# Splitting the next weights behind the eviction of the last finished product, in one encoder layer on one core

## The chip, the core and the metric

The kernel runs on one core of a Trainium2 chip. Five engines work side by side, each with a queue of its own that it takes in order: PE (TensorE, the matmuls), DVE (VectorE), ACT (ScalarE), POOL (GpSimd) and SP (SyncE, which here issues most DMAs). An engine that meets an instruction whose inputs are not ready waits with everything behind it. The metric is the time of one execution on the device, in microseconds (us). It was 2259.2, 2258.1 and 2256.8 us in three runs, a median of 2258.14 us.

## What is computed

One layer of an encoder, in float32, on two inputs with the same weights: `x_prompt` (1024 tokens of width 1024), called A below, and `x_sample` (512 tokens), called B. Cut to what matters:

```python
def encoder_layer(x, ...):
    h = rms_norm(x, pre_w)
    cols = h @ w_in                       # q|k, v, o, z, gates of the mLSTM; q, k, v, z of the attention; merge gates
    m_qk, m_v, m_o, m_z, m_i, m_f, a_qkv, a_z, gate = split(cols)
    y_m = mlstm_mixer(m_qk, m_v, m_o, m_i, m_f, ...) * silu(m_z)     # both directions, chunks of 128 tokens
    y_a = dilated_attention(a_qkv, rel_table) * silu(a_z)            # 3 dilations, 8 heads of 64
    p_m = y_m @ w_proj_m
    p_a = y_a @ w_proj_a
    g = sigmoid(gate)
    merged = g[0] * p_m + g[1] * p_a
    return x + rms_norm(merged @ w_out, post_w)
```

The mLSTM is a recurrence over chunks: each step takes a matrix state (`cf` in the kernel), adds the product of keys and values of the chunk to it, and divides by a denominator that follows from it.

## The kernel before

[...] Each operand is held as a high part, rounded, and a low part, the rest; `mm3` (L206) issues high × high, high × low and low × high (lines L209, L210, L211), and leaves out low × low.

**Weights.** A tile of weights is 128 x 1024 float32. `load_w` (L255) has it brought by a DMA into one of two buffers `wraw`; the queue is SP's, and POOL's in the later stages. `split_w` (L264) makes the high part with ACT (L272, `wh`) and the low part with DVE (L278, `wl`), into one of three pairs of buffers (in some stages there are more: `X0`, `X1`, `Q1`). Loading and splitting run two tiles of weights ahead of the products.

**Products.** `unit` (L792) multiplies one tile of weights with the activations of 512 tokens: 8 steps of `mm3` into one PSUM bank called `dense`, of which the scans' stage has two. Then `use(ps)` evicts the finished product, that is, ACT or DVE read the bank and so give it back: `silu` (ACT's tanh, L746, and DVE's product, L749 or L751), `att_unit` (ACT's copy, L772, and DVE's low part, L774), `conv` (ACT's copy, L870), `gate` (ACT's tanh, L896), and in the last stages `proj_m`, `proj_a` and `close`.

**Stages.** To about 950 us the projections of A with `w_in`, with a scheme of products of their own; from 973 to 1330 us the scan of A's mLSTM, with the projections of B set between its steps; to about 1600 us the attention of A with further projections; then the scan of B (to about 1830 us); then the attention of B beside the products with `w_proj_m` and `w_proj_a` (`w_pm`, `w_pa`), and the last product with `w_out`.

**A step of the scan** takes `rm` (POOL L1103, ACT L1105, DVE L1106), `sch`/`scl` (ACT L1109, POOL L1110), `kh`/`kl` (ACT L1124, DVE L1125), `qh`/`ql` (ACT L1117, POOL L1118); PE then writes `num` (two PSUM banks) and `kv` (one). DVE reads `kv` into the state `cf` (L1149, L1152); ACT and DVE read `num` into `X` (L1167, L1169), with a reciprocal `r` (L1163, L1164); ACT and DVE then split the state again (`ch` L1176, `cl` L1177). `hn` (ACT L1182, L1185) and `r` (POOL L1183, L1184) norm the heads.

**A step of the attention** takes the logits `lg` (PE L1362), their maximum with a bias into `ls` and `ot` (DVE L1374, `ISA` in the lists below), `nm` (DVE L1376), the exponential (ACT L1378), a transpose (`pt`, PE L1385), its copy (`pts`, ACT L1388 or DVE L1390) and the product `o` (PE L1398). `K0`, `K1` are the high and low part of rows `ymr` that POOL loads (L250, L1594, L1595).

**What sets the order.** The order on PE and on SP is that of the code, written by hand. On ACT, DVE and POOL a scheduler sets it, which takes each instruction's turn from a model of the timeline. `issue_after(x)` gives it a further condition: what is issued under it comes after `x`. Between instructions of one engine that is a place in the queue and costs no semaphore. `split_w` uses it already: both parts come after the instructions in `self.held` (in the attention, the last four steps' reads of PSUM), the low part also after those in `self.scans` (in the scan, the last reads of `kv` and `num`).

Of the kernel before, what the change touches and what calls it, by code (L numbers as in the profile page):

```python
# [22 lines left out]
F32 = mybir.dt.float32  # L23
# [158 lines left out]
class Net:  # L182
    def __init__(self, tc, a):
        self.tc, self.nc, self.a = tc, tc.nc, a
        self.clock = self.lag = 0
        self.pending, self.owner = [], {}
        self.defer, self.mixed, self.rows = False, set(), {}
        self.queued, self.pace = [], 1
        self.side = self.nc.sync
        self.lows = None  # L190
        self.scans, self.state, self.held, self.sum = [], [], [], None
        self.low_part = None
        self.retired = []
        self.narrow, self.acc, self.direct = {}, [None, None], {}
# [69 lines left out]
    def split_w(self, raw, n):  # L264
# [4 lines left out]
        with ExitStack() as st:  # L269
            for x in self.held:  # L270
                st.enter_context(self.tc.issue_after(x.ins))
            high = nc.scalar.activation(hi[:, :n], raw[:, :n], AF.Copy)  # L272

        def rest():
            with ExitStack() as st:
                for x in (*self.held, *self.scans):
                    st.enter_context(self.tc.issue_after(x.ins))
                low = (self.lows or nc.vector).tensor_sub(lo[:, :n], raw[:, :n], hi[:, :n].bitcast(F32))  # L278
# [463 lines left out]
    def silu(self, c, g, w):  # L742

        nc = self.nc
        th = w()
        nc.scalar.activation(th, c, AF.Tanh, scale=0.5)  # L746
        if g is None:
            g = th
            nc.vector.scalar_tensor_tensor(g, th, 1.0, c, op0=OP.add, op1=OP.mult)  # L749
        else:  # L750
# [9 lines left out]
    def att_unit(self, j, c, T, w):  # L760
# [10 lines left out]
        for h, _, x in parts:  # L771
            nc.scalar.activation(h, x, AF.Copy, scale=1.0 if keys else 0.125)  # L772
        for h, l, x in parts:
            nc.vector.scalar_tensor_tensor(l, x, 1.0 if keys else 0.125, h.bitcast(F32), op0=OP.mult, op1=OP.subtract)  # L774
        self.put(("aqk", T.S, j), T.aqk[0, j], hi.bitcast(F32), hi)
# [86 lines left out]
    def short_units(self, T):  # L862
# [5 lines left out]
        def conv(u):  # L868
            def use(p):
                nc.scalar.activation(self.sraw[:, 1:1 + BLK], p, AF.Copy)  # L870
                self.conv_unit(u, T, self.sraw, w, False)
# [21 lines left out]
        def gate(br, ct):  # L893
            def use(p):
                t = w()
                nc.scalar.activation(t, p, AF.Tanh, scale=0.5)  # L896
                self.put(("gt", T.S, br, ct), T.gt[br, ct], t, t)
# [719 lines left out]
    def branches(self, T, b, odd, before):  # L1617
# [12 lines left out]
        def proj_m(weights):  # L1630
            m2[:] = [self.place(1 - odd, i, F32) for i in (0, 2)]
            gate(1, 0)
            for ct in range(KT):
                wm = weights()
                pm = self.dense()
                for k in range(KT):
# [5 lines left out]
                    if k == KT - 1:  # L1642
                        nc.vector.scalar_tensor_tensor(m2[ct // 4][:, ct % 4], gates.pop((1, ct)), 1.0, pm, op0=OP.add, op1=OP.mult)  # L1643
                    yield

        def proj_a(weights):
            for ct in range(KT):
# [5 lines left out]
                for k in range(4):  # L1653
# [4 lines left out]
                    if k == 3:  # L1658
                        mg = self.osb.tile([P, BLK], F32, name="mg", bufs=2)
                        nc.vector.scalar_tensor_tensor(mg, gates.pop((0, ct)), 1.0, pa, op0=OP.add, op1=OP.mult)  # L1660
                        nc.vector.tensor_add(mg, mg, m2[ct // 4][:, ct % 4])
# [20 lines left out]
    def final(self, T, b):  # L1682
# [4 lines left out]
        def make(weights):  # L1687
# [13 lines left out]
            def close(u, t, c, p):  # L1701
                r0 = b * BLK + t * P
                o1 = sb.tile([P, BLK], F32, name="mg", bufs=2) if u else o[t]
                nc.scalar.activation(o1, p, AF.Square, accum_out=ss[:, t, u:u + 1])
                if u == 0:
                    nc.vector.tensor_mul(o[t], p, pw[:, c])
                    return
                which, xt = xo[t]
                nc.vector.scalar_tensor_tensor(ss[:, t, 5:6], ss[:, t, 0:1], 4 * EPS * D, ss[:, t, 1:2], op0=OP.add, op1=OP.add)
                nc.gpsimd.tensor_tensor(ss[:, t, 6:7], ss[:, t, 5:6], self.mhalf[:, :1], op=OP.pow)  # L1710
                nc.vector.tensor_mul(o1, p, pw[:, c])
                for hf, x in enumerate((o[t], o1)):
# [338 lines left out]
```

## Time and profile before

| | |
|---|---|
| median of three runs | 2258.14 us |
| the profiled execution | 2261.5 us, its span 2259.7 us |
| PE busy | 2244.2 us, 99% of the span |
| DVE, ACT, POOL busy | 1509.5, 1129.2 and 718.6 us |
| bytes moved by DMA | 418.27 MB, 185 GB/s |

The span is the time from the first to the last instruction that the profiler recorded; 1.8 us of the execution lie around it. An instruction in the trace has a start, a duration, its engine, its line and what it writes and reads; the names of buffers are shown without their numbers there. In square brackets stands the idle time of the engine ahead of it, with what ended it. PE's idle time is the difference of its busy time and the span, 15.5 us in all.

### The profile page before, as it was taken

The numbers are of one execution on the slowest core, as the hardware profiler recorded it, in microseconds if no ns is written. First come the engines' busy times: TensorE is split into PE (matmuls) and PEld (weight loads), VectorE is DVE, ScalarE is ACT, GpSimd is POOL, SyncE is SP. The second block draws the span as 40 slices with busy tenths as digits, with TensorE's granted clock in tenths as the row PEclk, the third lists the DMA queues.
The fourth block names the chain that finished last, engine by engine and source line by source line (L and its number), as shares of the span: only waits on it lengthen the run. The fifth ranks groups of instructions, "written<-read, shape, count | busy, mean of one in ns | idle before, by whom it ended". The sixth has DMA issues, their size and how long they took to land.

```text
span 2259.7 us, 35388 instructions
## 1 busy us (share of the span) xinstructions
PE 2244.2 (99%) x12226; PEld 1964.6 (87%) x12226; DVE 1509.5 (67%) x2875; ACT 1129.2 (50%) x2369; POOL 718.6 (32%) x1000
## 2 busy tenths in 40 slices
PE   9999999999999999999999999999999999999998
PEld 8999888888888888888888899999888888888887
DVE  7765577687776556558887755544689844655674
ACT  6432244344444434357777655566665644554332
POOL 1000333333333223237676610011165522221221
PEclk9999999999999999999999999999999999999999
DMA  3652455543332223284664789997678797776663
GB/s 123 168 134 76 172 205 192 192 176 121 112 111 103 84 84 140 103 298 153 226 223 127 191 217 235 253 245 221 203 248 284 238 278 211 233 251 200 233 230 109
DMA packets 222685, 418.27 MB, mean 185 GB/s; under 512 B 24841, under 2 KB 128969, under 8 KB 222506
## 3 DMA queue, kind: packets, MB, share of 16 engines
q1 hardware_dynamic: 194536, 315.86, 44.4%
q0 software_dynamic: 24368, 87.56, 12.4%
q10 hardware_dynamic: 3602, 12.59, 1.4%
q8 instruction: 97, 1.59, 0.3%
q14 instruction: 82, 0.67, 0.1%
HBM read 296.19 MB, written 128.12 MB: 188 GB/s over the span
## 4 chain that ended last, share of the span: by engine, by line
PE 95%; DMA 2%; issue 1%; ACT 1%; POOL 1%; DVE 0%; DVEq 0%; SPq 0%; POOLq 0%; ACTq 0%
PE d L211 14%; PE d L209 14%; PE d L210 14%; PE dense L209 12%; PE dense L211 12%; PE dense L210 12%; PE o L1398 4%; PE pt L1385 2%; PE lg L1362 2%; PE num L211 1%; PE num L209 1%; PE num L210 1%; PE kv L209 1%; PE a L1070 1%; PE kv L210 1%
## 5 line engine op out<-in xcount | busy, mean ns | idle before, releaser
L209 PE MATMUL dense<-H,wh 128*128 128x512 f32 x664 | 270.6, 408 | 0.8 <-DVE V0b L1643 0.8
L211 PE MATMUL dense<-H,wl 128*128 128x512 f32 x664 | 260.9, 393 | 0.0
L210 PE MATMUL dense<-H,wh 128*128 128x512 f32 x664 | 260.2, 392 | 0.0
L210 PE MATMUL d<-Hl,phla 128*128 128x512 f32 x608 | 236.5, 389 | 0.0
L211 PE MATMUL d<-Hh,phla 128*128 128x512 f32 x608 | 236.5, 389 | 0.0
L209 PE MATMUL d<-Hh,phla 128*128 128x512 f32 x608 | 236.5, 389 | 0.0
L278 DVE TENSOR_TENSOR wl<-wraw,wh 128x1024 fp32r<-128x1024 f32 (+1 forms) x121 | 149.3, 1234 | 70.0 <-ACT wh L272 69.9
L1374 DVE CUSTOM_DVE_ANT_0 ls<-lg,bias 128x256 f32<-128x256 f32 (+1 forms) x288 | 93.7, 362 | 132.8 <-PE lg L1362 71.2
L211 PE MATMUL d<-Hh,phlb 128*128 128x512 f32 x456 | 177.4, 389 | 0.0
L209 PE MATMUL d<-Hh,phlb 128*128 128x512 f32 x456 | 177.4, 389 | 0.0
L210 PE MATMUL d<-Hl,phlb 128*128 128x512 f32 x456 | 177.4, 389 | 0.0
L687 POOL TENSOR_TENSOR psum_w<-pw_raw 128x512 f32<-128x512 f32 x38 | 58.0, 1527 | 365.1 <-DMA pw_raw<-w_in 208.8
L1378 ACT ACTIVATE ls<-ls,nm 128x256 f32<-128x256 f32 (+1 forms) x288 | 130.3, 454 | 84.0 <-DVE nm L1376 59.2
L272 ACT ACTIVATE wh<-wraw 128x1024 fp32r<-128x1024 f32 (+1 forms) x124 | 128.7, 1038 | 77.1 <-PE dense L210 27.0
L211 PEld LDWEIGHTS dense<-H,wl 128*128 128x128 f32 x664 | 124.6, 188 | 28.2
L209 PE MATMUL d<-vhi,Hh 128*128 128x322 f32 x448 | 140.9, 315 | 0.3
L211 PE MATMUL d<-vhi,Hl 128*128 128x322 f32 x448 | 140.3, 313 | 0.4 <-DVE Hl L396 0.2
L210 PE MATMUL d<-vlo,Hh 128*128 128x322 f32 x448 | 139.7, 312 | 0.0
L209 PEld LDWEIGHTS dense<-H,wh 128*128 128x128 f32 x664 | 125.0, 188 | 15.5 <-DVE V0b L1643 1.2
L210 PEld LDWEIGHTS dense<-H,wh 128*128 128x128 f32 x664 | 125.4, 189 | 14.3
L211 PEld LDWEIGHTS d<-Hh,phla 128*128 128x128 f32 x608 | 114.1, 188 | 23.7
L210 PEld LDWEIGHTS d<-Hl,phla 128*128 128x128 f32 x608 | 114.2, 188 | 23.6
(570 smaller groups left out, 6166.4 us busy)
## 6 DMA issues: line engine op xcount, KB each, us to landing
pw_raw<-w_in SPq DMA_DIRECT2D x76, 512.0 KB
wraw<-w_in SPq DMA_DIRECT2D x64, 512.0 KB
aqk_a<-pwk SPq DMA_DIRECT2D x48, 512.0 KB
aqk_b<-sw SPq DMA_DIRECT2D x48, 256.0 KB
wraw<-w_pm POOLq DMA_DIRECT2D x24, 512.0 KB, 6.1
wraw<-w_out POOLq DMA_DIRECT2D x24, 512.0 KB, 4.0
wraw<-w_v POOLq DMA_DIRECT2D x22, 430.0 KB, 7.3
erep<-erow SPq DMA_DIRECT2D x16, 512.0 KB
```

The lines of the kernel that those rows point to most:

```text
L209: nc.tensor.matmul(out, lh, rh, start=start, stop=False)
L210: nc.tensor.matmul(out, lh, rl, start=False, stop=False)
L211: nc.tensor.matmul(out, ll, rh, start=False, stop=stop)
L272: high = nc.scalar.activation(hi[:, :n], raw[:, :n], AF.Copy)
L278: low = (self.lows or nc.vector).tensor_sub(lo[:, :n], raw[:, :n], hi[:, :n].bitcast(F32))
L687: self.nc.gpsimd.tensor_add(s[:, 0], ws[1][:, 0], ws[1][:, 1])
L1070: nc.tensor.matmul(p[:, c - c0], kT[:, ct, c * P:(c + 1) * P], qT[:, ct, c * P:(c + 1) * P], start=ct == 0, stop=ct == 1)
L1362: nc.tensor.matmul(lg[:, hh, c:c + w], q[hh][:, qs], z[:, k0:k0 + w], start=z is k[hh], stop=z is not k[hh])
L1374: nc.vector.tensor_tensor_reduce(out=ls[:, hh], in0=ts["lg"][hh], in1=bt[:, hh], scale=1.0, scalar=NEG, op0=OP.add, op1=OP.max, accum_out= ...
L1378: self.held = self.held[-3:] + [nc.scalar.activation(ls[:, hh], ls[:, hh], AF.Exp, bias=nm[:, hh:hh + 1], accum_out=ot[:, 128 + hh:129 + hh])]
L1385: nc.tensor.transpose(pp[:, hh * nk + x], ts["ls"][:, hh, x * P:(x + 1) * P], self.ident)
L1398: nc.tensor.matmul(po[:, hh * 64:hh * 64 + 64], pt[:, hh * nk + x], v[:, kt[x], c0 + hh * 64:c0 + hh * 64 + 64], start=x == 0, stop=x == n ...
```

## The change

A new list `self.evicted` holds the instructions on ACT and DVE that evict the last finished product. Each `use` sets it anew. `split_w` puts both the high part and the low part behind what the list holds, in addition to `held` and `scans`. Since the condition is only one of order on the same engine, the high part comes after ACT's entries and the low part after DVE's.

```diff
--- before.py
+++ after.py
@@ -189,7 +189,7 @@
         self.side = self.nc.sync
         self.lows = None
         self.scans, self.state, self.held, self.sum = [], [], [], None
-        self.low_part = None
+        self.low_part, self.evicted = None, []
         self.retired = []
         self.narrow, self.acc, self.direct = {}, [None, None], {}
 
@@ -267,13 +267,13 @@
         hi, lo = self.wsplit.pop(0)
         self.wsplit.append((hi, lo))
         with ExitStack() as st:
-            for x in self.held:
+            for x in (*self.held, *self.evicted):
                 st.enter_context(self.tc.issue_after(x.ins))
             high = nc.scalar.activation(hi[:, :n], raw[:, :n], AF.Copy)
 
         def rest():
             with ExitStack() as st:
-                for x in (*self.held, *self.scans):
+                for x in (*self.held, *self.evicted, *self.scans):
                     st.enter_context(self.tc.issue_after(x.ins))
                 low = (self.lows or nc.vector).tensor_sub(lo[:, :n], raw[:, :n], hi[:, :n].bitcast(F32))
             self.splits = high, low
@@ -743,10 +743,10 @@
 
         nc = self.nc
         th = w()
-        nc.scalar.activation(th, c, AF.Tanh, scale=0.5)
+        self.evicted = [nc.scalar.activation(th, c, AF.Tanh, scale=0.5)]
         if g is None:
             g = th
-            nc.vector.scalar_tensor_tensor(g, th, 1.0, c, op0=OP.add, op1=OP.mult)
+            self.evicted.append(nc.vector.scalar_tensor_tensor(g, th, 1.0, c, op0=OP.add, op1=OP.mult))
         else:
             nc.vector.scalar_tensor_tensor(g, th, 1.0, g, op0=OP.add, op1=OP.mult)
         return g
@@ -769,9 +769,10 @@
             by = lambda z: z.rearrange("p (r i) -> p r i", r=dil)
             parts = [(by(hi), by(lo), c.rearrange("p (i r) -> p r i", r=dil))]
         for h, _, x in parts:
-            nc.scalar.activation(h, x, AF.Copy, scale=1.0 if keys else 0.125)
+            self.evicted = [nc.scalar.activation(h, x, AF.Copy, scale=1.0 if keys else 0.125)]
         for h, l, x in parts:
-            nc.vector.scalar_tensor_tensor(l, x, 1.0 if keys else 0.125, h.bitcast(F32), op0=OP.mult, op1=OP.subtract)
+            low = nc.vector.scalar_tensor_tensor(l, x, 1.0 if keys else 0.125, h.bitcast(F32), op0=OP.mult, op1=OP.subtract)
+        self.evicted.append(low)
         self.put(("aqk", T.S, j), T.aqk[0, j], hi.bitcast(F32), hi)
         self.put(("aqk", T.S, j), T.aqk[1, j], lo.bitcast(F32), lo)
 
@@ -867,7 +868,7 @@
 
         def conv(u):
             def use(p):
-                nc.scalar.activation(self.sraw[:, 1:1 + BLK], p, AF.Copy)
+                self.evicted = [nc.scalar.activation(self.sraw[:, 1:1 + BLK], p, AF.Copy)]
                 self.conv_unit(u, T, self.sraw, w, False)
             return self.unit(u, use)
 
@@ -893,7 +894,7 @@
         def gate(br, ct):
             def use(p):
                 t = w()
-                nc.scalar.activation(t, p, AF.Tanh, scale=0.5)
+                self.evicted = [nc.scalar.activation(t, p, AF.Tanh, scale=0.5)]
                 self.put(("gt", T.S, br, ct), T.gt[br, ct], t, t)
             return self.unit((U_GB, U_GA)[br] + ct, use)
 
@@ -1640,7 +1641,8 @@
                     if k == 3:
                         gate(*((1, ct + 1) if ct < KT - 1 else (0, 0)))
                     if k == KT - 1:
-                        nc.vector.scalar_tensor_tensor(m2[ct // 4][:, ct % 4], gates.pop((1, ct)), 1.0, pm, op0=OP.add, op1=OP.mult)
+                        self.evicted = [nc.vector.scalar_tensor_tensor(m2[ct // 4][:, ct % 4], gates.pop((1, ct)), 1.0, pm,
+                                                                       op0=OP.add, op1=OP.mult)]
                     yield
 
         def proj_a(weights):
@@ -1657,7 +1659,7 @@
                         gate(0, ct + 1)
                     if k == 3:
                         mg = self.osb.tile([P, BLK], F32, name="mg", bufs=2)
-                        nc.vector.scalar_tensor_tensor(mg, gates.pop((0, ct)), 1.0, pa, op0=OP.add, op1=OP.mult)
+                        self.evicted = [nc.vector.scalar_tensor_tensor(mg, gates.pop((0, ct)), 1.0, pa, op0=OP.add, op1=OP.mult)]
                         nc.vector.tensor_add(mg, mg, m2[ct // 4][:, ct % 4])
                         nc.scalar.activation(mh[:, ct % 4], mg, AF.Copy)
                         nc.vector.tensor_sub(ml[:, ct % 4], mg, mh[:, ct % 4].bitcast(F32))
@@ -1701,14 +1703,14 @@
             def close(u, t, c, p):
                 r0 = b * BLK + t * P
                 o1 = sb.tile([P, BLK], F32, name="mg", bufs=2) if u else o[t]
-                nc.scalar.activation(o1, p, AF.Square, accum_out=ss[:, t, u:u + 1])
+                self.evicted = [nc.scalar.activation(o1, p, AF.Square, accum_out=ss[:, t, u:u + 1])]
                 if u == 0:
-                    nc.vector.tensor_mul(o[t], p, pw[:, c])
+                    self.evicted.append(nc.vector.tensor_mul(o[t], p, pw[:, c]))
                     return
                 which, xt = xo[t]
                 nc.vector.scalar_tensor_tensor(ss[:, t, 5:6], ss[:, t, 0:1], 4 * EPS * D, ss[:, t, 1:2], op0=OP.add, op1=OP.add)
                 nc.gpsimd.tensor_tensor(ss[:, t, 6:7], ss[:, t, 5:6], self.mhalf[:, :1], op=OP.pow)
-                nc.vector.tensor_mul(o1, p, pw[:, c])
+                self.evicted.append(nc.vector.tensor_mul(o1, p, pw[:, c]))
                 for hf, x in enumerate((o[t], o1)):
                     c2 = slice(hf * BLK, (hf + 1) * BLK)
                     nc.vector.scalar_tensor_tensor(xt[hf], x, ss[:, t, 6:7], xt[hf], op0=OP.mult, op1=OP.add)
```

The names below have the buffers' numbers, and lines after the change are one or two higher than before (L1185 is L1186).

On ACT at about 1057 us of the profile before, in the scan of A, where `wh0` is the high part of the next weights, `sw2` the eviction of a product and `hn3` a step of the head norm, there stood

```order
L1182 ACTIVATE hn3_7909,r_8888<-X0_7911 128x256
L1109 ACTIVATE sch_8994<-rm_8988 128x128
L272 ACTIVATE wh0_7755<-wraw0_7753 128x1024
L772 ACTIVATE sw2_7873<-dense_8805 128x512
L1185 ACTIVATE hn3_7909<-X0_7911,r_8888 128x256
L1105 ACTIVATE rm_9107<-rm_9107,col1024_715 128x128
L1124 ACTIVATE kh_9117<-K1_8196,col1024_715 128x256
```

and now stand

```order
L1183 ACTIVATE hn3_7909,r_8888<-X0_7911 128x256
L1110 ACTIVATE sch_8994<-rm_8988 128x128
L772 ACTIVATE sw2_7873<-dense_8805 128x512
L1186 ACTIVATE hn3_7909<-X0_7911,r_8888 128x256
L272 ACTIVATE wh0_7755<-wraw0_7753 128x1024
L1106 ACTIVATE rm_9107<-rm_9107,col1024_715 128x128
L1125 ACTIVATE kh_9117<-K1_8196,col1024_715 128x256
```

The eviction now comes ahead of the split, and so does the second `hn3`; the rows behind are the same. On DVE at about 1287 us, late in the same scan, where `sg` is the eviction's second half (it reads ACT's `sw3`) and `cf1` the state, there stood

```order
L1163 SCALAR_TENSOR_TENSOR r_12057<-num_12030,col1024_715 128x1
L1164 RECIPROCAL r_12057<-r_12057 128x1
L1169 SCALAR_TENSOR_TENSOR X0_7911<-num_12030,r_12057,X0_7911 128x256
L1177 TENSOR_TENSOR cl0_12062<-cf0_11384,ch0_12061 128x516
L1152 SCALAR_TENSOR_TENSOR cf1_11444<-cf1_11444,rw1_7903,kv_12105 128x516
L751 SCALAR_TENSOR_TENSOR sg_7877<-sw3_7874,sg_7877 128x512
L1125 SCALAR_TENSOR_TENSOR kl_12155<-K1_10377,col1024_715,kh_12154 128x256
```

and now stand

```order
L1164 SCALAR_TENSOR_TENSOR r_12057<-num_12030,col1024_715 128x1
L1165 RECIPROCAL r_12057<-r_12057 128x1
L1170 SCALAR_TENSOR_TENSOR X0_7911<-num_12030,r_12057,X0_7911 128x256
L1178 TENSOR_TENSOR cl0_12062<-cf0_11384,ch0_12061 128x516
L751 SCALAR_TENSOR_TENSOR sg_7877<-sw3_7874,sg_7877 128x512
L1153 SCALAR_TENSOR_TENSOR cf1_11444<-cf1_11444,rw1_7903,kv_12105 128x516
L1164 SCALAR_TENSOR_TENSOR r_12125<-num_12092,col1024_715 128x1
L1126 SCALAR_TENSOR_TENSOR kl_12155<-K1_10377,col1024_715,kh_12154 128x256
```

`sg` now stands ahead of `cf1` instead of behind it. On ACT at 1839 to 1855 us, in the attention of B beside the products with `w_pm`, where `wh0` to `wh2` are high parts of such weights, `sw0` to `sw2` evictions of the gates' products, and `ls` the exponentials of the steps `ot1` to `ot3`, there stood

```order
L272 ACTIVATE wh1_7757<-wraw0_7753 128x1024
L896 ACTIVATE sw0_7871<-dense_18811 128x512
L1378 ACTIVATE ls_18906,ot1_18786<-ls_18906,nm_18907 128x256 x2
L1594 ACTIVATE K0_18817<-ymr0_18770 128x512
L1378 ACTIVATE ls_18955,ot2_18787<-ls_18955,nm_18956 128x256 x2
L896 ACTIVATE sw1_7872<-dense_18879 128x512
L272 ACTIVATE wh2_7759<-wraw1_7754 128x1024
L1388 ACTIVATE pts_18967<-pt_18962 128x512
L272 ACTIVATE wh0_7755<-wraw0_7753 128x1024
L1378 ACTIVATE ls_19001,ot3_18788<-ls_19001,nm_19002 128x256 x2
```

and now stand

```order
L897 ACTIVATE sw0_7871<-dense_18811 128x512
L1379 ACTIVATE ls_18906,ot1_18786<-ls_18906,nm_18907 128x256 x2
L1595 ACTIVATE K0_18817<-ymr0_18770 128x512
L1379 ACTIVATE ls_18955,ot2_18787<-ls_18955,nm_18956 128x256 x2
L272 ACTIVATE wh1_7757<-wraw0_7753 128x1024
L897 ACTIVATE sw1_7872<-dense_18879 128x512
L272 ACTIVATE wh2_7759<-wraw1_7754 128x1024
L1389 ACTIVATE pts_18967<-pt_18962 128x512
L272 ACTIVATE wh0_7755<-wraw0_7753 128x1024
L897 ACTIVATE sw2_7873<-dense_18939 128x512
L1401 ACTIVATE ot0_18785<-o_18783 128x128
L1379 ACTIVATE ls_19001,ot3_18788<-ls_19001,nm_19002 128x256 x2
```

`sw0` has moved ahead of `wh1`, and `wh1` behind the exponentials of two steps; the exponentials of `ot3` have moved behind one more eviction and a copy. The same on DVE, with the low parts `wl1`, `wl2` and `wl0`; there stood

```order
L278 TENSOR_TENSOR wl1_7758<-wraw0_7753,wh1_7757 128x1024
L1374 ISA ls_18955,ot2_18787<-lg_18901,bias0_18795 128x256
L1374 ISA ot2_18787 128x1
L1374 ISA ls_18955,ot2_18787<-lg_18901,bias0_18795 128x256
L1374 ISA ot2_18787 128x1
L1390 COPY pts_18917<-pt_18784 128x512
L1376 TENSOR_SCALAR nm_18956<-ot2_18787 128x2
L1595 TENSOR_TENSOR K1_18818<-ymr0_18770,K0_18817 128x512
L278 TENSOR_TENSOR wl2_7760<-wraw1_7754,wh2_7759 128x1024
L1374 ISA ls_19001,ot3_18788<-lg_18946,bias1_18796 128x256
L1374 ISA ot3_18788 128x1
```

and now stand

```order
L1391 COPY pts_18917<-pt_18784 128x512
L1377 TENSOR_SCALAR nm_18956<-ot2_18787 128x2
L278 TENSOR_TENSOR wl1_7758<-wraw0_7753,wh1_7757 128x1024
L278 TENSOR_TENSOR wl2_7760<-wraw1_7754,wh2_7759 128x1024
L278 TENSOR_TENSOR wl0_7756<-wraw0_7753,wh0_7755 128x1024
L1375 ISA ls_19001,ot3_18788<-lg_18946,bias1_18796 128x256
L1375 ISA ot3_18788 128x1
L1375 ISA ls_19001,ot3_18788<-lg_18946,bias1_18796 128x256
L1375 ISA ot3_18788 128x1
L1375 ISA ls_19061,ot4_18789<-lg_18996,bias2_18797 128x256
L1375 ISA ot4_18789 128x1
L1375 ISA ls_19061,ot4_18789<-lg_18996,bias2_18797 128x256
```

The three low parts have moved together, behind the copy `pts` and `nm` of an earlier step and ahead of the rows of the step `ot3`. On POOL, two loads of `ymr` have moved ahead of loads of `w_pm` in the same place.

## The prediction

> **What bounds the kernel now.** I read the page first, then the idle time of PE by what ended it, whole and in the two stretches where the change moves anything, then the instructions one by one around those waits. The page's first part gives the share of PE, and its second the clock:
>
> ```profile
> PE 2244.2 (99%) x12226; PEld 1964.6 (87%) x12226; DVE 1509.5 (67%) x2875; ACT 1129.2 (50%) x2369; POOL 718.6 (32%) x1000
> ...
> PEclk9999999999999999999999999999999999999999
> ```
>
> PE works for 2244.2 of 2259.7 us, at full clock. No edit of the order on ACT and DVE changes what PE has to do, so it can win at most a part of the 15.5 us in which PE is idle; losing is unbounded. The same view of waits, for 972 to 1335 us (the scan of A) and for 1600 to 1850 us (the scan of B and the first projections), which is where the instructions of ACT and DVE stand in another order than before:
>
> ```profile
> PE num L211 <- POOL scl L1110: 1.2, 1, 1.2
> PE kv L209 <- DVE cf L1152: 0.6, 1, 0.6
> PE kv L209 <- DVE r L1163: 0.4, 1, 0.4
> PE num L209 <- DVE X L1169: 0.2, 1, 0.2
> ...
> PE dense L209 <- ACT sw L896: 0.7, 1, 0.7
> PE kv L209 <- DVE cf L1152: 0.5, 1, 0.5
> PE kv L209 <- DVE cf L1149: 0.2, 1, 0.2
> ```
>
> The columns are the total, the number and the longest. Only one of these seven waits is for an eviction (`sw`, L896); the others are for the scan's own work. Before 972 us, from 1335 to 1600 us and after about 1865 us nothing moves, so whatever PE waits there stays. How full the two helpers are in the scan:
>
> ```profile
> 972.00:1330.00 358.00, 355.54 (x2103) 312.50 (x2102) 271.77 (x551) 239.93 (x572) 220.67 (x347) 1.00 0.64 202
> 1660.00:1830.00 170.00, 169.29 (x972) 147.28 (x971) 144.17 (x313) 99.59 (x236) 93.80 (x154) 1.00 0.77 249
> ```
>
> After the stretch and its length come PE, the weight loads, DVE, ACT, POOL, the granted clock and the DMA. DVE is at 76 and 85%, ACT at 67 and 59%: a moved instruction finds a hole somewhere, but what stands behind it may come late first.
>
> **The change part by part.** No instruction is added or removed, no semaphore either, and the order on PE and SP is the same; the edits to the code are thus costed by the places where the order differs. Most differ alike: ACT's split of the next weights, 1.05 us, and ACT's eviction of the product that just ended, 0.58 us, change places. Both had been ready at the same time.
>
> ```profile
> L272 ACT ACTIVATE wh<-wraw 128x1024 fp32r<-128x1024 f32 x109 | 114.9, 1054 | 62.7 <-PE dense L210 22.7 <-DMA wraw<-w_pm 14.8 <-DMA wraw<-w_in 8.5
> ```
>
> The 22.7 us idle until the end of a product of `dense` are this: the weights' slot comes free when the product is done, and so does the product. The swap brings the eviction 0.95 us forward (the spacing of the two starts) and the split 0.5 us back. A split is made two products ahead of its use, and one product of `dense` is 24 matmuls, started 0.23 us apart (1844.87 and 1845.10):
>
> ```profile
> 1844.87 0.39 PE L209 MATMUL dense<-H,wh 128*128 128x512 f32 x1
> 1845.10 0.39 PE L210 MATMUL dense<-H,wh 128*128 128x512 f32 x1
> ```
>
> So PE has at least 24 × 0.23 = 5.5 us of other work between a split and its use, and the delay of 0.5 us costs it nothing; that lead is the cover. In itself such a swap is worth nothing either, unless somebody waits for the eviction. Five places remain.
>
> *First, 1057 us.* On ACT the split also goes behind `hn` (L1185), which waits for POOL. Rows of ACT before, then POOL, DVE and PE:
>
> ```profile
> 1057.49 1.05 ACT L272 ACTIVATE wh<-wraw 128x1024 fp32r<-128x1024 f32 x1
> 1058.44 0.57 ACT L772 ACTIVATE sw<-dense 128x512 fp32r<-128x512 f32 x1
> 1059.11 0.51 ACT L1185 ACTIVATE hn<-X,r 128x256 f32<-128x256 f32 x1
> ...
> 1064.84 0.51 ACT L1185 ACTIVATE hn<-X,r 128x256 f32<-128x256 f32 x1 [1.03 <-POOL r L1184]
> ...
> 1066.04 0.74 POOL L1118 TENSOR_TENSOR ql<-qw,qh 128x256 fp32r<-128x256 f32 x1 [0.41 <-ACT qh L1117]
> ...
> 1081.54 0.69 DVE L1149 COPY cf<-kv 128x516 f32<-128x516 f32 x1
> ...
> 1082.35 0.32 PE L209 MATMUL kv<-V1a,kh 128*128 128x258 f32 x1
> ```
>
> The split sat in a hole in which ACT would have waited for POOL; now it starts after `hn`, which still starts at 1059.11, and everything behind is late by 0.95 us. ACT's idle time doesn't take that up: `hn` waits for POOL's `r`, and POOL's `ql` for ACT's `qh`, so the two pass the lag round. It reaches PE where the slack is small. The single bank of `kv` is free when DVE has read it: at 1081.54 + 0.69 = 1082.23, and PE writes it at 1082.35, a slack of 0.12 us. So +0.83, taken as **+0.9**, since the 0.12 is also used by DVE's own new order. Bounds: 0, if some hole takes the lag up in these 24 us, and 1.9, if it comes twice.
>
> *Second, 1283 and 1289 us.* Rows of DVE, of ACT and of PE:
>
> ```profile
> 1280.08 0.69 DVE L749 SCALAR_TENSOR_TENSOR sg<-sg,dense 128x512 f32<-128x512 f32 x1 [0.61 <-ACT sg L746]
> ...
> 1283.45 0.74 DVE L1152 SCALAR_TENSOR_TENSOR cf<-cf,rw,kv 128x516 f32<-128x516 f32 x1
> ...
> 1284.34 0.36 PE L209 MATMUL kv<-V1a,kh 128*128 128x258 f32 x1 [0.64 <-DVE cf L1152]
> ...
> 1287.41 1.05 ACT L272 ACTIVATE wh<-wraw 128x1024 fp32r<-128x1024 f32 x1
> 1288.36 0.58 ACT L746 ACTIVATE sw<-dense 128x512 f32<-128x512 f32 x1
> ...
> 1287.67 0.74 DVE L1152 SCALAR_TENSOR_TENSOR cf<-cf,rw,kv 128x516 f32<-128x516 f32 x1
> 1288.97 0.69 DVE L751 SCALAR_TENSOR_TENSOR sg<-sw,sg 128x512 f32<-128x512 f32 x1 [0.56 <-ACT sw L746]
> ...
> 1289.23 0.28 PE L209 MATMUL kv<-V1a,kh 128*128 128x258 f32 x1
> ```
>
> At 1280 DVE waits 0.61 us for the eviction; 0.95 us earlier, it waits for nothing, two small steps go behind `sg`, and `cf` comes some 0.45 us earlier. PE's wait of 0.64 falls to 0.2: −0.45. At 1287.67 the reverse: `sg` now stands ahead of `cf`. ACT's part ends near 1287.41 + 0.58 = 1287.99, `sg` runs until 1288.7 and `cf` until about 1289.4, 0.2 after PE's 1289.23: +0.2. Net **−0.25**; bounds −1.2 (all three waits of PE for DVE in that stretch, 0.6 + 0.4 + 0.2, gone) and +0.7 (a whole `sg` of 0.69 on the path).
>
> *Third, 1777 us.*
>
> ```profile
> 1776.47 0.29 DVE L1106 TENSOR_TENSOR rm<-rm,st 128x128 f32<-128x128 f32 x1 [1.30 <-ACT rm L1105]
> 1776.68 0.69 DVE L1149 COPY cf<-kv 128x516 f32<-128x516 f32 x1
> ...
> 1777.43 0.39 PE L209 MATMUL kv<-V1a,kh 128*128 128x258 f32 x1 [0.19 <-DVE cf L1149]
> ```
>
> `cf` now stands ahead of this `rm` and doesn't wait for ACT: **−0.2**, the whole wait; bounds −0.7 (the 0.5 for L1152 too) and 0.
>
> *Fourth, 1845 us,* the one wait for an eviction.
>
> ```profile
> 1844.84 1.06 ACT L272 ACTIVATE wh<-wraw 128x1024 fp32r<-128x1024 f32 x1 [4.68 <-DMA wraw<-w_pm]
> 1845.80 0.58 ACT L896 ACTIVATE sw<-dense 128x512 f32<-128x512 f32 x1
> ...
> 1846.43 0.50 PE L209 MATMUL dense<-H,X 128*128 128x512 f32 x1 [0.72 <-ACT sw L896]
> ```
>
> ACT stood 4.68 us in front of a split whose weights had not landed, and the finished product behind it. The eviction now goes ahead: **−0.7**, all of it. Bounds −0.7 and 0 (PE stopped by something else there).
>
> *Fifth, 1847 to 1861 us,* the price of the fourth. That split (`wh1`) now also stands behind `ls` of two steps, and its low part (`wl1`, on DVE) behind `pts` and `nm`; POOL's next load of w_pm waits until the low part has read its buffer. Further on, `ls` and the rows of the step `ot3` stand behind the split of that load, and PE transposes `ls` at 1860.66.
>
> ```profile
> 1847.45 0.54 POOL L261 DMA_DIRECT2D wraw<-w_pm  x1 [5.21 <-DMA gt_b<-sw]
> ...
> 1852.82 1.06 ACT L272 ACTIVATE wh<-wraw 128x1024 fp32r<-128x1024 f32 x1 [1.14 <-DMA wraw<-w_pm]
> ...
> 1860.66 0.60 PE L1385 MATMUL pt<-ident,ls 128*128 128x128 f32 x4
> ...
> DMA to landing us min/median/max: 3.8/6.5/10.1
> ```
>
> The load goes out 2 to 3 us later, say at 1850.0, and lands after 5.4 us as before (1847.45 to 1852.82): 1855.4. Then the high part (1.05), the low part (1.22), four rows of DVE on `lg` (0.34 each), a copy (0.69) and `nm` (0.2), and two `ls` on ACT (0.5 each): 5.5 us, 1860.9. With 6.5 us, the median landing of the loads from 1800 to 1900 us, 2.5 + 5.5 behind 1847.45 + 6.5 gives 1862.0. Between 0.2 and 1.3 late, I take **+0.7**. Bounds: 0 with a landing of 3.8 us, and +5.4 if both loads concerned land late, this one after the 10.1 us of the slowest.
>
> **Sum:** 0.9 − 0.25 − 0.2 − 0.7 + 0.7 = +0.45 us on the profiled execution of 2261.5 us, which stands 3.4 us above the median of the runs, 2258.1. I put it on the median: **2258.6 us**. With the terms' bounds, not all at one end, this case lies in 2256.9 to 2260.5. A measurement can tell about 0.2% from no change, 4.5 us here, so this is no change.
>
> **The rivals.**
> *Slower, by the fifth place alone.* What speaks for it: the split now holds back `ls`, which PE needs, where before it held back an eviction, and a landing of 10.1 us is in the rows. Against it: the median is 6.5. It goes past 0.2% from a landing of about 10 us on; PE then stands some 5 us: 2258.1 + 5.4 − 0.7 + 0.4 = 2263.2.
> *The clock falls after it.* The longest wait of PE is 2.3 us (`d` for the load of `prew`), and every slice shows the full clock; no row shows what follows a wait of 5 us:
>
> ```profile
> PE d L1803 <- DMA Hh<-prew: 2.3, 1, 2.3
> ```
>
> If PE ran at half clock for as long again as it stood, 5 us, it would lose another 2.5 us: 2265.7. Nothing in this trace speaks for that. [...]
> *Slower, by lags that add up.* In the scan of B, DVE is busy for 85%, and the same passing round as at 1057 us could take place there and again near 1280 us: four lags of 0.95 are 3.8 us, 2261.9. Against it: most of the swaps bring DVE's share of the eviction forward and leave the rest where it was.
> *Faster.* Evictions that come earlier empty DVE's queue in front of `cf`, `r` and `X`, and all PE's waits for ACT and DVE in the two stretches go: 0.6 + 0.4 + 0.2 + 0.7 + 0.5 + 0.2 = 2.6, 2255.5. Against it: only the 0.7 and the 0.64 are tied to an eviction by a row.
> *No effect.* PE's order is fixed and the lead of the splits long: 2258.1.
>
> **How the numbers follow.** The forecast 0.50; slower by the fifth place 0.11, with the clock 0.03; lags 0.14; faster 0.12; no effect 0.10. The range takes in faster (2255.5, and a little below it) and the fifth place (2263.2, and a little above): 2255.2 to 2263.6, with about 0.15 left out, the clock among it. Below 2253.6 lies 0.03, from the tail of faster; above 2262.7 lie the 0.14 of the fifth place and the clock, and 0.02 of the lags: 0.16.
>
> **What would show it.** First: `wh` at 1059.5 and ACT, POOL and DVE 0.9 us late up to a wait of `kv` or `num` near 1078 to 1097 us. Second: the wait at 1284 at 0.2, a new one of `kv` at 1289. Third: none at 1777. Fourth: no wait of `dense` for `sw` at 1846, `sw` near 1840.2. Fifth: the load at about 1850, and a wait of `pt` for `ls` of 0 to 2 us at 1861. The prediction is wrong if PE shows a wait over 3 us, or any wait for the split weights themselves (`wh`, `wl`), whose lead I cost at nothing, or if it moves outside of the two stretches.

## The result, and the profile after

The changed kernel takes 2265.63 us in the median of 13 runs (2264.69 to 2268.49), beside 2258.45 us for the kernel before in 13 runs on the same chips. The ratio is 1.0032, with a 95% interval of 1.0025 to 1.0039: slower by 7.2 us, where 0.5 us was forecast and 2263.6 us was the upper end of the range. The profiled execution took 2264.89 us with a span of 2263.1 us.

The page's shares and its row of the clock, after:

```profile
PE 2245.0 (99%) x12226; PEld 1965.7 (87%) x12226; DVE 1509.1 (67%) x2875; ACT 1125.1 (50%) x2369; POOL 715.6 (32%) x1000
...
PEclk9999999999999999999999999999999999999999
```

They look like those of before; a place of 10 us doesn't show in shares of a span of 2263 us, nor in slices of 57 us. PE's idle time by what ended it (total, times, longest) shows it:

```profile
PE lg L1363 <- DVE ot L1375: 3.3, 1, 3.3
PE d L1805 <- DMA Hh<-prew: 2.3, 1, 2.3
PE num L211 <- POOL scl L1111: 0.9, 1, 0.9
...
PE pt L1386 <- ACT ls L1379: 0.8, 1, 0.8
PE num L209 <- ACT X L1168: 0.7, 1, 0.7
PE dense L209 <- ACT sw L897: 0.7, 1, 0.7
...
PE kv L209 <- DVE cf L1150: 0.4, 1, 0.4
```

The waits for `lg` and `pt`, 4.1 us, are new, and both belong to the fifth place of the prediction. The clock shows only in short stretches (start:end, length, PE, weight loads, DVE, ACT, POOL, granted clock, DMA share, GB/s):

```profile
1855.00:1860.00 5.00, 2.51 (x16) 2.10 (x14) 1.23 (x2) 1.71 (x3) 0.00 (x0) 0.99 0.77 173
1860.00:1865.00 5.00, 3.40 (x11) 2.70 (x12) 2.90 (x12) 2.86 (x9) 0.53 (x1) 0.50 0.87 249
1865.00:1870.00 5.00, 5.00 (x23) 4.09 (x22) 3.74 (x10) 4.78 (x13) 3.79 (x7) 0.83 0.94 298
```

After the wait PE runs at 0.50 and then 0.83 of its clock. That costs 3.40 × 0.50 + 5.00 × 0.17 = 2.55 us more. The rows of that place, POOL, ACT, DVE and PE:

```profile
1850.39 0.53 POOL L261 DMA_DIRECT2D wraw<-w_pm  x1 [4.17 <-DVE wl L278]
...
1857.68 1.06 ACT L272 ACTIVATE wh<-wraw 128x1024 fp32r<-128x1024 f32 x1 [6.39 <-DMA wraw<-w_pm]
...
1862.65 0.49 ACT L1379 ACTIVATE ls<-ls,nm 128x256 f32<-128x256 f32 x1
...
1858.77 1.23 DVE L278 TENSOR_TENSOR wl<-wraw,wh 128x1024 fp32r<-128x1024 f32 x1 [6.13 <-ACT wh L272]
1859.91 0.42 DVE L1375 CUSTOM_DVE_ANT_0 ls<-lg,bias 128x256 f32<-128x256 f32 x1
...
1860.25 0.42 DVE L1375 CUSTOM_DVE_ANT_0 ls<-lg,bias 128x256 f32<-128x256 f32 x1
...
1860.83 1.20 PE L1363 MATMUL lg<-V1a,Q 128*128 128x256 f32 x4 [3.32 <-DVE ot L1375]
1862.80 1.18 PE L1386 MATMUL pt<-ident,ls 128*128 128x128 f32 x4 [0.77 <-ACT ls L1379]
```

The load went out at 1850.39 and its split began at 1857.68, 7.3 us later. DVE stood 6.13 us in front of the low part, with the reads of logits that had been ready since 1846 behind it. PE wanted to write the next logits at 1857.5; `lg` has two banks, both held by logits that nobody had read. In the kernel before, the first of these reads stood ahead of the late low part, and PE didn't wait (DVE, PE):

```profile
1852.38 0.42 DVE L1374 CUSTOM_DVE_ANT_0 ls<-lg,bias 128x256 f32<-128x256 f32 x1
...
1860.10 0.72 PE L1362 MATMUL lg<-V1a,Q 128*128 128x256 f32 x4
```

The 12226 matmuls stand in the same order in both traces, so PE's start of each can be compared one by one. How far it was ahead (−) or behind (+) of the trace of before:

| stretch of before, us | change of PE's lead there, us | the prediction's term |
|---|---|---|
| start to 1056 | −0.80 | none |
| 1056 to 1100 | +0.94 | first: +0.9 |
| 1262 to 1295 | −2.03 | second: −0.25 |
| 1296 to 1730 | −0.06 | none |
| 1730 to 1780 | −0.80 | third: −0.2 |
| 1837 to 1848 | −0.03 | fourth: −0.7 |
| 1857 to 1870 | +6.86 | fifth: +0.7 |
| 1870 to the end | −0.69 | none |
| sum | +3.39 | +0.45 |

The sum agrees with the two spans, 2263.1 − 2259.7. It is less than the 7.2 us of the medians, because the profiled execution of before lay 3 us above its median. The trace of `row_behind` below, which has the order of before but for one place, shows where: its PE is ahead of that trace by 1.0 us after the first 12 us, by 1.4 at 998 us and again at 1475, and by another 1.0 us at 2026 us, where before waits 0.8 us for `V0b`; its span is 2257.4 us. Against it the changed kernel is 5.7 us longer; 6.85 us are lost at 1857 to 1870 us, after a lead of only 1.3 us there, not the 2.8 us that it has against the trace of before.

### The profile page after: what moved, and what is told of

Its sections match the earlier page's. It is cut to its first block, busy times and chain, and to the rows that moved or that the text cites. A ratio compares the mean times of both kernels' runs of the same rounds, so it can differ in the third digit from the quotient of the medians.

```text
span 2263.1 us, 35332 instructions
## 1 busy us (share of the span) xinstructions
PE 2245.0 (99%) x12226; PEld 1965.7 (87%) x12226; DVE 1509.1 (67%) x2875; ACT 1125.1 (50%) x2369; POOL 715.6 (32%) x1000
## 4 chain that ended last, share of the span: by engine, by line
PE 89%; DMA 5%; issue 2%; DVE 2%; ACT 1%; POOL 1%; SPq 0%; DVEq 0%; POOLq 0%; ACTq 0%
PE d L211 13%; PE d L210 13%; PE d L209 13%; PE dense L209 11%; PE dense L211 11%; PE dense L210 11%; PE o L1399 3%; PE pt L1386 2%; PE lg L1363 1%; PE num L211 1%; PE num L209 1%; PE num L210 1%; DMA ymr<-ym_a 1%; DMA vs_a<-vz 1%; PE a L1071 1%
## 5 line engine op out<-in xcount | busy, mean ns | idle before, releaser
L211 PEld LDWEIGHTS d<-Hh,phla 128*128 128x128 f32 x608 | 114.2, 188 | 23.7
L209 PEld LDWEIGHTS d<-Hh,phla 128*128 128x128 f32 x608 | 114.2, 188 | 23.6
```

The lines of the kernel that those rows point to most:

```text
L209: nc.tensor.matmul(out, lh, rh, start=start, stop=False)
L211: nc.tensor.matmul(out, ll, rh, start=False, stop=stop)
```

## The experiments

### Which half of the change: `scan_only` and `rest_only`

The new condition holds only while a scan is under way (`scan_only`, below), or only while none is (`rest_only`, with `not self.scans`):

```diff
+        evicted = self.evicted if self.scans else []
         with ExitStack() as st:
-            for x in (*self.held, *self.evicted):
+            for x in (*self.held, *evicted):
...
-                for x in (*self.held, *self.evicted, *self.scans):
+                for x in (*self.held, *evicted, *self.scans):
```

> The new condition holds only while a scan of the mLSTM is under way; the order from the end of the second scan on (about 1830 us) is that of before. Theory (the loss is one place, 1857 to 1867 us, where DVE read the logits too late: 4.1 us of idle PE and about 2.5 us at half clock): without that place the kernel is 6.6 us below the changed one, 2259.0, or lower by the scans' own gain; in the two profiles PE gained 1.3 us in the scan of A and 0.8 us in that of B, so 2256.4 to 2259; granted clock 1.000. Rival (lags of ACT in the scans make the loss, and what is seen at 1860 us is only where they surface): 2263 or more.

Measured: 2261.62 us, ratio 1.0015 (1.0006 to 1.0024). Neither: 2.6 us above the theory's upper end, 1.4 below the rival. Rows of ACT and PE, then two stretches:

```profile
1842.88 1.06 ACT L273 ACTIVATE wh<-wraw 128x1024 fp32r<-128x1024 f32 x1 [2.35 <-DMA wraw<-w_pm]
1843.84 0.58 ACT L898 ACTIVATE sw<-dense 128x512 f32<-128x512 f32 x1
...
1844.47 0.63 PE L209 MATMUL dense<-H,X 128*128 128x512 f32 x1 [2.38 <-ACT sw L898]
```

```profile
1840.00:1845.00 5.00, 2.62 (x12) 1.79 (x11) 2.33 (x3) 2.65 (x6) 0.53 (x1) 0.97 1.05 278
1845.00:1850.00 5.00, 5.00 (x23) 4.31 (x22) 2.27 (x8) 3.47 (x10) 2.30 (x5) 0.69 1.04 405
```

In this trace the scans gained: PE reaches 1845 us of before 3.6 us early, and 2.3 us ahead of the trace of `row_behind`. There the order is that of before, an eviction behind a split that waits for its load, and the load landed only 2.0 us earlier than in before (1842.88 for 1844.84). The wait of 0.72 us became 2.38, and PE then ran at 0.69 of its clock over 5 us, about 1.6 us more (1.7 by the length of the slow stretch, shown below). So a second place can do what the fifth does, and in this trace time won ahead of it is spent there.

> The opposite half: the new condition holds everywhere but in the two scans. Theory of the one place: all of the loss, 2265 to 2266, granted clock 0.998, and a wait of the logits of over 3 us near 1860 us. Rival (lags in the scans): 2258 to 2260.

Measured: 2262.37 us, ratio 1.0020 (1.0010 to 1.0029). Less than the theory's 2265, more than the rival's 2260. The waits, then a stretch:

```profile
PE pt L1387 <- ACT ls L1380: 1.3, 1, 1.3
PE lg L1364 <- DVE ot L1376: 0.7, 1, 0.7
```

```profile
1860.00:1865.00 5.00, 4.16 (x19) 3.30 (x20) 2.86 (x10) 4.87 (x14) 1.23 (x2) 1.00 1.04 275
```

The same two waits at the same place, 2.0 us in place of 4.1, and in this execution no slow clock. The load took 7.2 us here too (1848.43 to 1855.66), but it went out 2.0 us earlier than in the changed kernel, and PE came 0.65 us later; so the smaller wait comes mostly from the earlier load, and only in small part from gains of the scans that are missing. Over its 10 runs the kernel spreads from 2260.2 to 2265.8 us.

### What at the fifth place: `row_first`, `row_behind`, `both_first`

`row_first` is the changed kernel, with the low part of that one split (the 103rd) issued behind DVE's reads of the logits of step `ot3`:

```diff
-        if self.scans:
+        if self.scans or self.nsplit == 103:
             self.low_part = rest
...
-                    nc.vector.tensor_tensor_reduce(out=ls[:, hh], in0=ts["lg"][hh], in1=bt[:, hh], scale=1.0, scalar=NEG,
+                    top = nc.vector.tensor_tensor_reduce(out=ls[:, hh], in0=ts["lg"][hh], in1=bt[:, hh], scale=1.0, scalar=NEG,
...
+                if self.nsoft == 100:
+                    with self.tc.issue_after(top.ins):
+                        self.rest()
```

> The changed kernel with one instruction moved: at the place near 1857 us the low part of the late weights is put behind DVE's two reads of the logits of step ot3, so that these no longer stand behind a load. All loads are as late as in the changed kernel. Theory (the loss needs both, a late load and the reads of the logits behind it): the wait goes, granted clock 1.000, 2258.5 to 2259.5. Rival 1 (the lateness of the loads costs by itself, through the weights): 2262 or more, PE waiting for a product of dense. Rival 2 (the exponentials behind the same split on ACT hold up the transposes all the same): a wait of pt of 1 to 2 us is left, 2260 to 2261.

Measured: 2262.52 us, ratio 1.0022 (1.0013 to 1.0031). The wait for `lg` is gone, but what follows is rival 2, larger than it said:

```profile
1855.84 1.06 ACT L273 ACTIVATE wh<-wraw 128x1024 fp32r<-128x1024 f32 x1 [5.51 <-DMA wraw<-w_pm]
...
1858.33 0.51 ACT L1384 ACTIVATE ls<-ls,nm 128x256 f32<-128x256 f32 x1 [0.78 <-DVE nm L1382]
...
1858.98 0.93 PE L1391 MATMUL pt<-ident,ls 128*128 128x128 f32 x4 [2.75 <-ACT ls L1384]
```

```profile
1860.00:1865.00 5.00, 5.00 (x16) 3.98 (x15) 4.33 (x9) 5.00 (x16) 2.93 (x6) 0.66 0.98 278
```

The exponentials still stand behind the high part, and the `nm` that they need behind the low part. PE's wait has moved from `lg` to `pt` and is still 2.75 us, with 5.00 × 0.34 = 1.7 us of slow clock.

`row_behind` is the opposite: the kernel before, with only those reads put behind that low part.

```diff
+            if self.nsplit == 103:
+                self.hold_soft = low
...
-                for hh in range(2):
+                with self.tc.issue_after(self.hold_soft.ins) if self.nsoft == 100 else ExitStack():
+                    for hh in range(2):
```

> The kernel before with only the other half: DVE's reads of the logits of step ot3 are put behind the low part of those weights, whose load is as early as before (landed at 1852.8, low part done at 1855.1). Theory (both are needed): the reads end near 1856, 4 us ahead of the logits at 1860.1 that need the bank; no change, 2258.5, clock 1.000. Rival (that place in the queue is enough, since a landing varies by several us from run to run): 2262 or more in the median, or times that scatter between 2258 and 2265.

Measured: 2258.35 us, ratio 1.0002 (0.9993 to 1.0011), no wait at that place. Rows of DVE and PE:

```profile
1852.65 1.23 DVE L279 TENSOR_TENSOR wl<-wraw,wh 128x1024 fp32r<-128x1024 f32 x1 [1.69 <-ACT wh L273]
1853.80 0.42 DVE L1379 CUSTOM_DVE_ANT_0 ls<-lg,bias 128x256 f32<-128x256 f32 x1
1854.14 0.42 DVE L1379 CUSTOM_DVE_ANT_0 ls<-lg,bias 128x256 f32<-128x256 f32 x1
...
1858.61 0.72 PE L1365 MATMUL lg<-V1a,Q 128*128 128x256 f32 x4
```

The reads end 4 us before PE needs the bank. Here, with the load early, the place behind it costs nothing; the theory holds.

`both_first` is the changed kernel with both parts of that split behind the whole of step `ot3`, reads and exponentials; `both` issues the high and then the low part, and the second piece stands behind the exponentials:

```diff
+        if self.nsplit == 103:
+            self.rest()
+            self.low_part = both
+            return hi[:, :n], lo[:, :n]
...
+                self.nsoft += 1
+                if self.nsoft == 100:
+                    self.rest()
```

> The changed kernel, with the high and the low part of the late weights both behind step ot3: its reads of the logits on DVE and its exponentials on ACT come first. Theory A (two things stood behind that one load, the reads and the exponentials, and the first trial moved the reads alone and left a wait of pt of 2.8 us and the slow clock after it): the wait and the slow clock go, 4.7 us of the profile, so 2262.5 - 4.7 = 2257.8, granted clock 1.000. Rival B (PE, now 3 us ahead of before, always finds some load that has not landed, since the DMA engines are full from 1840 to 1865 us): another wait of 1 to 3 us shows up right after, 2260 to 2262.

Measured: 2258.69 us, ratio 1.0001 (0.9992 to 1.0010). PE does not wait at all from 1835 to 1900 us, and the clock is full:

```profile
1855.00:1860.00 5.00, 5.00 (x32) 4.43 (x31) 2.65 (x12) 2.15 (x5) 1.17 (x3) 1.00 1.04 315
1860.00:1865.00 5.00, 5.00 (x31) 4.37 (x30) 2.84 (x6) 3.03 (x8) 0.94 (x2) 1.00 1.06 325
```

One split in another place gives back all but 0.6 of the 7.2 us (before took 2258.09 us beside it), and rival B's next wait doesn't come, though the DMA engines are full (shares of 1.04 and 1.06). Without that place the change makes no difference that these runs can tell.

`rows_too` adds the new condition to the high parts of the rows `ymr` as well:

```diff
-                    nc.scalar.activation(hi[:, k - 2, :w], t[:, :w], AF.Copy)
+                    with ExitStack() as st:
+                        for x in self.evicted:
+                            st.enter_context(self.tc.issue_after(x.ins))
+                        nc.scalar.activation(hi[:, k - 2, :w], t[:, :w], AF.Copy)
```

> As both_first, and the high parts of the rows ymr also go behind the evictions, so that no eviction waits for a load of ymr. Theory A: the wait of 0.7 us of dense for sw near 1837 us goes as well, 2257.1 if both_first gives 2257.8. Rival B (each load moved back holds up something else): 2260 or more.

Measured: 2258.31 us, ratio 0.9998 (0.9989 to 1.0007). The wait of `dense` for `sw` is not there, as it isn't in the trace of `both_first`; against the kernel before it is no gain that could be told. No version here is faster than the kernel before.

### One part alone: `low_only`

With the condition on the high part alone the order on every engine is, row for row, that of the full change; on the low part it adds nothing, since a low part comes after its high part anyhow. The low part alone:

```diff
-            for x in (*self.held, *self.evicted):
+            for x in self.held:
```

> One part of the change alone: only the low part on DVE comes behind the evictions, the high part on ACT stays. Theory (all of the effect is in ACT's order, since with the condition on the high part alone the order of every engine is that of the full change): 2258 to 2259, no new wait of PE above 1 us. Rival (DVE's order matters by itself): a difference of over 2 us either way.

Measured: 2259.53 us, ratio 1.0005 (0.9995 to 1.0014). No difference that can be told. All of the effect comes with the high part on ACT, and what moves on DVE follows from it.

### What a wait of PE costs: `stall14`, `stall16`, `stall20`

The kernel before, with copies on DVE ahead of its reads of the logits of step `ot3`:

```diff
+                for _ in range(20 if self.nsoft == 100 else 0):
+                    nc.vector.tensor_copy(ls, bt)
```

> The disputed cost by itself, on the kernel before: 20 copies of 128x512 are added on DVE ahead of its reads of the logits of step ot3, and nothing else; they write a tile that those reads overwrite. From the spacing of 0.6 us of a DVE copy of that shape in the profile the reads come about 12 us later than 1852.4, at 1864, PE stands at the logits of 1860 for some 4 to 5 us. Theory (a stall of that length halves the clock for about as long): the loss is the idle time plus 2 to 2.5 us, with the granted clock near 0.5 to 0.7 in the 5 us behind it. Rival (the slow clock belongs to the changed order, not to the stall): the idle time alone, clock 1.00.

> As stall20, with 14 copies. One copy took 0.46 us in that run, so the reads come 2.7 us earlier and PE's wait of 4.46 us falls to about 1.7. Theory (the slow clock comes only after a long wait; so far 2.38 us had it in one trace and 1.25 us did not in another): clock 1.00 or a few per cent below in the 5 us after it, little or no loss beside the wait. Rival (each wait costs clock in proportion, 0.6 us for 1 us): about 1 us of slow clock.

> As stall20, with 16 copies: a wait of about 2.6 us. Theory (a long wait is followed by a time at half clock whose length does not depend much on the wait): 1.4 to 2.7 us lost beside the wait. Rival (in proportion): 1.6 us; so this run alone doesn't tell them apart, with 14 and 20 copies it does.

The waits of `stall14`, `stall16` and `stall20`, each from its own trace, and the stretch or stretches after each:

```profile
1857.96 0.93 PE L1388 MATMUL pt<-ident,ls 128*128 128x128 f32 x4 [0.89 <-ACT ls L1381]
```

```profile
1860.00:1865.00 5.00, 5.00 (x32) 4.40 (x31) 4.59 (x8) 3.67 (x11) 4.02 (x8) 1.00 1.06 306
```

```profile
1858.92 0.93 PE L1388 MATMUL pt<-ident,ls 128*128 128x128 f32 x4 [1.20 <-ACT ls L1381]
```

```profile
1860.00:1865.00 5.00, 5.00 (x29) 4.26 (x28) 4.54 (x5) 4.46 (x14) 3.09 (x6) 1.00 1.08 310
```

```profile
1861.88 1.18 PE L1388 MATMUL pt<-ident,ls 128*128 128x128 f32 x4 [4.46 <-ACT ls L1381]
```

```profile
1860.00:1865.00 5.00, 3.12 (x10) 2.44 (x11) 2.49 (x12) 3.78 (x12) 0.19 (x1) 0.61 0.83 234
1865.00:1870.00 5.00, 5.00 (x21) 4.07 (x19) 3.45 (x4) 2.14 (x5) 4.02 (x8) 0.70 0.65 200
```

`stall20` took 2265.33 us in its one run, with the order of before elsewhere, and its one long wait has the slow clock behind it. So the slow clock belongs to the wait, not to the change. `stall14` and `stall16` (2258.86 and 2259.52 us, one run each) got shorter waits than expected, 0.89 and 1.20, and the full clock after them; the 2.6 us that `stall16` was to probe wasn't reached.

Stretches of 5 us blur where the slow clock begins and ends. Cut at the changes of the clock that the traces record, the slow stretches of `scan_only`, `row_first`, the changed kernel and `stall20`, each from its own trace, are:

```profile
1844.69:1848.10 3.41, 3.41 (x12) 2.82 (x12) 2.58 (x8) 2.62 (x10) 2.30 (x5) 0.50 1.05 411
```

```profile
1860.23:1863.65 3.42, 3.42 (x10) 2.68 (x9) 3.21 (x8) 3.42 (x11) 1.65 (x2) 0.50 0.91 251
```

```profile
1859.86:1866.69 6.83, 5.09 (x15) 4.02 (x16) 4.70 (x19) 4.55 (x13) 1.44 (x3) 0.50 0.88 267
```

```profile
1861.14:1867.97 6.83, 6.09 (x16) 4.74 (x17) 4.10 (x7) 5.92 (x16) 2.70 (x5) 0.50 0.67 189
```

The granted clock is 0.50 in all four, and they last 3.41, 3.42, 6.83 and 6.83 us. In the traces of the changed kernel and of before, the changes of the clock lie whole multiples of 3.413 us after its first record of full speed (542, 544 and 659 of them in the changed kernel, 658 in before). So the table asks how long PE stood idle within one such step of 3.41 us, beside how long a wait was. The loss is an estimate from the clock of 0.50, half of PE's busy time in the slow stretch; in `stall20` the matmuls of 128x512 start 0.43 us apart there and 0.23 us apart behind it:

| wait of PE, us | kernel | most idle time in one step of 3.41 us | slow stretch, us | lost to the clock, us |
|---|---|---|---|---|
| 0.89 | stall14 | 0.71 | none | 0 |
| 1.20 | stall16 | 1.21 | none | 0 |
| 0.66 and 1.25 | rest_only | 1.31 | none | 0 |
| 2.38 | scan_only | 2.38 | 3.41 | 1.7 |
| 2.75 | row_first | 2.21 | 3.41 | 1.7 |
| 3.32 and 0.77 | changed kernel | 2.35 | 6.83 | 2.55 |
| 4.46 | stall20 | 3.41 | 6.83 | 3.05 |

Of the steps in the table, those with 2.21 us or more of idle time were followed by the clock of 0.50 and those with 1.31 us or less were not; what lies between was not measured. At the end of the kernel, steps with 3.41 us (before) and 2.50 us (changed kernel) were followed by it, and one with 1.30 us (before) was not. In the four slow stretches above, the step ahead of the return to the full clock had no idle time; a slow step with 1.74 us of it (changed kernel) or 0.73 us (`stall20`) was followed by a second one. This speaks against a loss in proportion that begins with the first microsecond. Three of the four slow stretches came behind a step in which PE still worked for 1.0 to 1.2 us.

## Why the prediction was wrong, by its own steps

*First place, +0.9:* right. PE lost 0.94 us from 1056 to 1100 us, most of it in the new wait of `num` for ACT's `X`, 0.7 us. The other traces bear it out: the four further kernels with the new order of ACT in that scan lose 0.96 to 0.98 us there, and the six without it (`rest_only`, `low_only`, `row_behind` and the three with copies) lose nothing there.

*Second place, −0.25, bounds −1.2 and +0.7:* the right sign, mis-sized. It measured −2.0. All three waits for DVE in that stretch went, 1.2 us by the view of waits; the new wait at 1289 us, set at +0.2, did not come. Not all of it need be the change's: the trace of `rest_only`, with the old order there, is also 1.0 us quicker than that of before in this stretch.

*Third place, −0.2:* the right sign, mis-sized: −0.80, past its bound of −0.7. The wait of 0.5 us at 1745 us went too, and a new one of 0.36 us for L1150 came at 1737.

*Fourth place, −0.7:* failed. The eviction at 1845 us did move ahead and its wait went, but the same wait came up one product earlier. Rows of ACT and PE in the changed kernel:

```profile
1836.09 0.63 ACT L1595 ACTIVATE K<-ymr 128x512 fp32r<-128x512 f32 x1 [6.22 <-DMA ymr<-ym_a]
1836.63 0.58 ACT L897 ACTIVATE sw<-dense 128x512 f32<-128x512 f32 x1
...
1837.26 0.50 PE L209 MATMUL dense<-H,wh 128*128 128x512 f32 x1 [0.69 <-ACT sw L897]
```

In the new order the split `X0` and the eviction ahead of it stand behind a `K0` that waits for rows `ymr`. I had looked at what the eviction was freed from, and not at what now stood in front of the one before it. The condition put the eviction ahead of a split, and the eviction still stood behind a load. The net was about nothing, −0.03. In the trace of `rest_only`, with the same order there, that wait didn't occur, and PE won 1.0 us: ACT stood 1.3 us in front of that `K0` and not 6.2.

*Fifth place, +0.7, bounds 0 and +5.4:* this is the step that failed. It was the right place and the right chain behind the late load, but the size was 6.9 us: 4.1 us of wait and 2.55 us of half clock, the rest in no single wait. Three things were mis-sized. The load took 7.3 us where I set 5.4 to 6.5 (1.9 and 0.8 less). PE arrived 2.8 us early by the trace of before (1.3 us by that of `row_behind`), by the gains of the places before and a quicker start; I had set the chain against PE's old time of 1860.66, as if those gains were kept. And the wait has the slow clock behind it, 2.55 us, which I had put into a rival of 0.03. The wait of 2.3 us for `prew` that I had named beside that rival could not speak on it: it stands from 0 to 2.28 us, ahead of the first record of the clock at 12.1 us. What came after the landing was right: 5.5 us from the split to the last exponential by the prediction, 1857.68 to 1863.1 in the trace. The wait that I had named, `pt` for `ls`, was 0.77 us; the reads of `lg`, which I had not counted as a limit of their own, stopped PE first, for 3.32 us. `row_first` shows that taking them away leaves a wait of 2.75 us; both had to go.

The sum's form was at fault too: five terms added as if each stood alone. Against a load that lands when it lands, time won before it is waited away; the trace of `scan_only` shows that, 2.3 to 3.6 us ahead by 1845 us, and the kernel is 3.2 us slower in the median. Whether the load landed late because the DMA engines were full (shares from 0.77 to 1.05 around it) was not tried: in the trace of before, the landings of loads of this size from 1800 to 1900 us run from 3.8 to 10.1 us, at shares from 0.52 to 1.02 over 20 us.

*The rivals.* The fifth place alone, with the clock falling after it, had 0.03, and is what happened. That its figure, 2265.7 us, stands 0.1 us from the median is luck: it was made of a wait of 5 us after a landing of 10.1 us, and the trace has 4.1 us after 7.3, with PE early. The half clock for as long as the wait was my assumption, from no row; the changed kernel has 6.83 us at 0.50 after its 4.1 us of waits. *Lags that add up* (0.14) did not happen: after the first place there is none. *Faster* (0.12) was right that all the waits for DVE of the first scan go. It isn't shown that this is worth a time: `both_first` spends nothing at the fifth place, and is no faster than the kernel before.

*What would show it wrong* was named as a wait of over 3 us, and that was the sign.

## What to carry to other kernels

Before an instruction that waits for a DMA is moved ahead of others in an engine's queue, count everything that comes to stand behind it, down to the PSUM banks that stay unread, and set it against the time at which PE will then arrive, with the gains ahead of it taken off. A gain ahead of a place that a load times is worth nothing until that place has slack. And price the waits of PE by more than their length: here those of 2.38 to 4.46 us cost 1.7 to 3.05 us more through the clock, and those up to 1.25 us nothing.

## What was not expected of the hardware

In the traces of before and of the changed kernel the granted clock changed only at whole multiples of 3.41 us, and a step need not be idle throughout: 2.21 us of idle time in it (`row_first`) were followed by a clock of 0.50, 1.31 us (`rest_only`) were not. So the price of the waits measured here is neither fixed nor in proportion: it is 0, or half of PE's busy time over 3.41 or 6.83 us, 1.7 to 3.05 us. Loads of 128 x 1024 float32 took from 3.8 to 10.1 us to land within one trace (before, 1800 to 1900 us). And executions with the same order differ by about 1 us within the first 13 us: PE's matmuls of 128 x 128 begin at 6.84 us both in before and in the changed kernel, and at 12.3 us the changed kernel is 0.96 us ahead. They start 0.21 us apart at first and 0.11 us apart later; the change comes at 12.1 us in before and at 9.8 us in the changed kernel, where each trace has its first record of the full clock, and 2.2 us at about half the pace account for about that difference. The single profile of before stands 3 us off its median in a kernel of 2258 us.
